# A hybrid decoder layer on one core: the fourth tile of the first queries moved into the stretch in which x lands

## The chip, the cores and the metric

The kernel runs on one core of one Trainium2 chip. The metric is device microseconds (us) of one execution, and the value to be predicted is the median over several executions of the changed kernel. The engines that matter here are TensorE (PE in the profile, with its weight loads as PEld), VectorE (DVE), ScalarE (ACT), GpSimd (POOL) and SyncE (SP), which issues most of the transfers.

## The reference, cut to what matters

One layer is computed for 512 tokens of width 1,024: a norm, one wide projection, gated linear attention, dilated attention in three groups, a merge, an MLP and a gated embedding. What the change touches is the first lines of it:

```
h = x * rsqrt(mean(x * x) + EPS) * ln1
q0, k0, q1, k1, ... = columns of h @ w_in      # group 0: queries q0, keys k0, four heads of 128 columns
logits0 = q0 @ k0^T / sqrt(128) + bias0        # needed later, once k0 and the bias tiles are there
```

## The kernel before

Every product of two fp32 matrices is made from three matmuls of a faster kind: each operand is split into a high part (`hi`, a copy on ACT) and a low part (`lo`, a subtraction on DVE), and high by high, high by low and low by high are added up in PSUM. A matmul here takes 128 rows of weights and streams 512 columns (the tokens).

**The start.** x arrives transposed, in eight chunks of 128 features by 512 tokens (`xr[k]`). Beside chunk k comes `wr[k]`, a piece of the tensor `ws`: the 128 rows of `w_in` for that chunk, for the first NS = 3 tiles (heads) of q0, and in a last column the norm's weight `ln1` for these features. SP issues ws 0, x 0, ws 1, x 1 and so on. For each k, ACT makes the high part of the weights (L465) and of x times `ln1` (L359) and a square of x (L390); DVE makes the low parts (L467, L367) and sums the squares (L472); PE then does 3 matmuls for each of the 3 tiles, which is 9 (L477 to L479, the second one of a tile needs the low part of x). The sum of squares is not needed yet: 1 / rms (`rstd`) is multiplied in when a finished tile is read out of PSUM (`qk0_evac`, L610). Eight matmuls on a tile of ones (L452) run before x is there.

**After the start.** The fourth tile of q0 and the four tiles of k0 are ordinary units: a weight tile `w` of 128 by 1,024 is loaded by SP (L201), split by `fetch` (L244 on ACT, L239 on DVE, up to two units ahead of use), and used by 24 matmuls in `fm` (L258). All of them use the splits of x that were made at the start.

**What sets the order.** The program is written out engine by engine in the order in which the Python code runs. `run` emits 8 matmuls and then calls `step`, which advances one of the generators in the list `side` by one yield. At this place `side` holds `setup` (the sum of squares into `rstd`: four small matmuls L397, a power on POOL, a diagonal tile that is split, and two matmuls L420 and L421 that spread it; then a small projection L560; then three small matmuls L577 for the bias tables, each with a copy on DVE, L579, and a store; then the loads that spread the tables into bias tiles, L595 and L597), and `renorm`, which makes for each of the eight chunks x times `ln1` times `rstd` (L497 on DVE), its high part (L357 on ACT) and its low part (L365 on DVE). From q1 on, all products use these normalized chunks `xs`. What is left in `side` after k0 is emitted by `drain()` in one piece, without matmuls between.

Each engine works its own list in order: an instruction that waits holds up all behind it on its engine. PSUM has eight banks, four for the large products (`mmt`) and four for small ones (`smt`), each handed out in turn.

```
side.append(setup())
q0t = fm("q0.3", xsr, ps=smt())
q0 = [qk0_evac(p, HD_SCALE) for p in q0ps + [q0t]]
k0 = [qk0_evac(fm(f"k0.{j}", xsr), 1.0) for j in range(4)]
drain()
side.append(xsums())
q1 = qk_cls("q1", HD_SCALE)
```

Of the kernel before, what the change touches and what calls it, by code (L numbers as in the profile page):

```python
# [10 lines left out]
F32 = mybir.dt.float32  # L11
F32R = mybir.dt.float32r
I32 = mybir.dt.int32
AF = mybir.ActivationFunctionType
OP = mybir.AluOpType
# [4 lines left out]
P = 128  # L20
T = 512
D = 1024
KC = D // P
EPS = 1e-6
NEG = -1e30
HD_SCALE = 128 ** -0.5


NS = 3


GQ, GK, GV, GR, GHA, ATT, GATE = 0, 512, 1024, 2048, 3072, 3088, 7696
# [2 lines left out]
def att_col(g, which):  # L35
    return ATT + (g * 3 + which) * 512
# [10 lines left out]
def weight_units():  # L47

    u = []

    def fm(name, src, col, n, row=0):
        for j in range(n):
            u.append((f"{name}.{j}", "fm", src, row, col + j * P))

    def tm(name, src, col):
        for i in range(4):
            u.append((f"{name}.{i}", "tm", src, i * 2 * P, col))

    fm("q0", "w_in", att_col(0, 0), 4)
    u = u[NS:]  # L60
    def quad(name, src, col, kind="quad", chunk=0):
        for m, k in ((0, 0), (1, 0), (1, 1), (0, 1)):
            u.append((f"{name}.A{m + 1}{k + 1}", kind, src, 2 * chunk + k, col + m * (P if kind == "quad" else 256)))

    fm("k0", "w_in", att_col(0, 1), 4)
    fm("q1", "w_in", att_col(1, 0), 4)
    quad("k1", "w_in", att_col(1, 1))
    quad("q2", "w_in", att_col(2, 0))
    quad("k2", "w_in", att_col(2, 1))
    quad("v1", "w_in", att_col(1, 2), "quadt")  # L70
    quad("v2", "w_in", att_col(2, 2), "quadt")
    quad("v0", "w_in", att_col(0, 2), "quadt")
    quad("gq", "w_in", GQ)
    quad("gk", "w_in", GK)
    quad("gv0", "w_in", GV, "quadt")
    for j in range(4):
        u.append((f"oa.{j}", "half", "w_o_attn", 0, j * 2 * P))
    quad("r0", "w_in", GR)
    quad("gv1", "w_in", GV + 512, "quadt")
    quad("r1", "w_in", GR + 512)  # L80
    for i in range(2):
        quad(f"gb{i}", "w_in", GATE + D + i * 512)
    for i in range(2):
        quad(f"ga{i}", "w_in", GATE + i * 512)
    fm("og", "w_o_gla", 0, 8)
    fm("wo", "w_out", 0, 8)
    for q in range(8):
        quad(f"m1q{q}", "w_mlp1", q * 512)
    for what, sub, c in MLP2:
        if what == "plain":  # L90
            for kk in range(4 * c, 4 * c + 4):
                u.append((f"m2s{sub}.{kk}", "tm", "w_mlp2", kk * 2 * P, sub * 512))
        else:
            quad(f"m2s{sub}c{c}", "w_mlp2", sub * 512, chunk=c)
    for j in range(2):
        u.append((f"pp{j}.0", "tm", "w_pp", 0, j * 512))
    for j in range(2):
        tm(f"pg{j}", "w_pg", j * 512)
    return u
# [35 lines left out]
C_LN2, C_LN3, C_BA, C_GN, C_LN1, C_LO, C_N = 0, 8, 16, 20, 28, 36, 38  # L135
# [14 lines left out]
def block_kernel(ctx, tc, xT, ws, pT, wts, wha, wa2, vec, lnf, rel, onehot, ident_d, mask_d, out):  # L150
    nc = tc.nc
    V, S, TE, SY, GP = nc.vector, nc.scalar, nc.tensor, nc.sync, nc.gpsimd

    const = ctx.enter_context(tc.tile_pool(name="const", bufs=1))
# [9 lines left out]
    def u32(name="u"):  # L164
        return ar.tile([P, T], F32, tag="u", name=name)
# [7 lines left out]
    def smt():  # L173
        return sm.tile([P, T], F32, tag="sm", name="smt")
# [76 lines left out]
    def weight(name, ahead=NW - 3):  # L251
        fetch(OPERAND[name] + ahead)
        return ready[name]
# [14 lines left out]
    def cols(t, c):  # L268
        return t[0][:, c], t[1][:, c]

    def fm(name, rhs, off=0, w=None, ps=None):

        w = w or weight(name)
        ps = ps or mmt()
        run(three(ps, [(cols(w, slice(off + i * P, off + (i + 1) * P)), rhs[i]) for i in range(len(rhs))]))
        return ps
# [151 lines left out]
    mh = const.tile([P, 4], F32, name="mh")  # L428
    V.memset(mh, -0.5)
    warm = const.tile([P, 4], F32, name="warm")  # L430
    S.activation(warm, mh, AF.Copy)
    xr, wr = [], []
    for k in range(KC):
        t = u32()
        SY.dma_start(t[:, 0:NS * P + 1], ws[k])
        wr.append(t)
        t = u32()
        SY.dma_start(t, xT[k * P:(k + 1) * P, :])
        xr.append(t)
    ident = const.tile([P, P], F32, name="ident")  # L440
    SY.dma_start(ident, ident_d)
    cv = const.tile([P, C_N], F32, name="cv")
    SY.dma_start(cv, vec)
    whs = const.tile([P, KC, 32], F32, name="whs")
    SY.dma_start(whs, wha)
    ones = const.tile([P, P], F32, name="ones")
# [11 lines left out]
    xsr = []  # L458
    acc, sq = None, None
    q0ps = [mmt() for _ in range(NS)]  # L460
    for k in range(KC):
        x, ln = xr[k], wr[k][:, NS * P:NS * P + 1]
        hi, lo = u32r(), u32r()
        c = slice(0, NS * P)
        S.activation(hi[:, c], wr[k][:, c], AF.Copy)  # L465
        xh = split_hi(x, ln)
        V.tensor_tensor(lo[:, c], wr[k][:, c], hi[:, c].bitcast(F32), op=OP.subtract)  # L467
        xsr.append(split_lo(x, xh, ln))
        if k == 1:
            acc = sq  # L470
        elif k > 1:
            V.tensor_tensor(acc, acc, sq, op=OP.add)  # L472
        sq = square(x)
        xh, xl = xsr[k]
        for i in range(NS):
            c = slice(i * P, (i + 1) * P)
            TE.matmul(q0ps[i], lhsT=hi[:, c], rhs=xh, start=k == 0, stop=False)  # L477
            TE.matmul(q0ps[i], lhsT=hi[:, c], rhs=xl, start=False, stop=False)  # L478
            TE.matmul(q0ps[i], lhsT=lo[:, c], rhs=xh, start=False, stop=k == KC - 1)  # L479
    V.tensor_tensor(acc, acc, sq, op=OP.add)  # L480
    for k in range(KC):
        V.tensor_scalar(whs[:, k, :], whs[:, k, :], wr[k][:, NS * P:NS * P + 1], None, op0=OP.mult)
    fetch(0)

    norm1, low, zin = [], [], []
# [121 lines left out]
    def qk0_evac(ps, scale):  # L607

        o = u32()
        V.scalar_tensor_tensor(out=o, in0=ps, scalar=scale, in1=norm1[1], op0=OP.mult, op1=OP.mult)  # L610
        return o
# [389 lines left out]


    side.append(setup())
    q0t = fm("q0.3", xsr, ps=smt())
    q0 = [qk0_evac(p, HD_SCALE) for p in q0ps + [q0t]]
    k0 = [qk0_evac(fm(f"k0.{j}", xsr), 1.0) for j in range(4)]
    drain()
    side.append(xsums())
    q1 = qk_cls("q1", HD_SCALE)
# [96 lines left out]
    for j in range(KC):  # L1106
        t = u32()
# [69 lines left out]
    for j in range(KC):  # L1177
        ps = fm(f"wo.{j}", mix)
# [166 lines left out]
    for i, (what, sub, c) in enumerate(MLP2):  # L1345
# [17 lines left out]
        if i == len(MLP2) - 2:  # L1363
            for k in range(2):
                t = u32()
                GP.dma_start(t, pT[k * P:(k + 1) * P, :])
                pt.append(split(t))
            for g in range(2):
                t = u32()
# [92 lines left out]
    for c in parts:  # L1462
        ps, n = mmt(), c.stop - c.start
# [37 lines left out]
def _layout(inputs):  # L1501
    f = {k: np.asarray(v) for k, v in inputs.items()}
    src = {k: f[k][0] for k in ("w_in", "w_o_gla", "w_o_attn", "w_out", "w_mlp1", "w_mlp2", "w_pp", "w_pg")}
    wts = np.empty((len(UNITS), P, 1024), np.float32)
    for i, (_, kind, s, r, c) in enumerate(UNITS):
        w = src[s]
        if kind == "fm":
            a = w[r:r + D, c:c + P].reshape(8, P, P).transpose(1, 0, 2)
        elif kind == "tm":
            a = w[r:r + 2 * P, c:c + 512].reshape(2, P, 512).transpose(1, 0, 2)  # L1510
        elif kind == "quadt":

            a = w.reshape(4, 2, P, -1)[:, r, :, c:c + 256].transpose(1, 0, 2)
        elif kind == "quad":

            a = w[r // 2 * D:(r // 2 + 1) * D].reshape(4, 2, P, -1)[:, r % 2, :, c:c + 3 * P]
            a = np.stack([a[..., :P], a[..., 2 * P:]], axis=2).transpose(1, 0, 2, 3)
        else:
            a = w[:, c:c + 256].reshape(4, P, 2, P).transpose(1, 2, 0, 3)
        wts[i] = a.reshape(P, 1024)  # L1520
    wha = np.zeros((P, KC, 32), np.float32)
    wha[:, :, :16] = src["w_in"][:, GHA:GHA + 16].reshape(KC, P, 16).transpose(1, 0, 2)
    wha[:, :, 16:] = wha[:, :, :16]
    wa2 = np.tile(f["w_a2"][0], (8, 1))
    vec = np.concatenate([v.reshape(-1, P).T for v in (f["ln2"][0], f["ln3"][0],
                                                       f["b_a"][0], f["gla_gn"][0], f["ln1"][0])]
                         + [np.tile(np.repeat(np.float32([[0, 1], [1, -1]]), 16, axis=0), (4, 1))], axis=1)
    c = att_col(0, 0)
    start = np.concatenate([src["w_in"][:, c:c + NS * P].reshape(KC, P, NS * P),
                            f["ln1"][0].reshape(KC, P, 1)], axis=2)  # L1530
    return {
        "xT": np.ascontiguousarray(f["x"][0].T),
        "ws": np.ascontiguousarray(start),
        "pT": np.ascontiguousarray(f["p"][0, 0].T),
        "wts": wts,
        "wha": wha,
        "wa2": wa2,
        "vec": np.ascontiguousarray(vec),
        "lnf": f["ln_f"].reshape(1, D),
        "rel": np.ascontiguousarray(f["rel_bias"]),  # L1540
        "onehot": _onehot(),
        "ident": np.eye(P, dtype=np.float32),
        "mask": np.triu(np.ones((P, P), np.int32)),
    }
# [16 lines left out]
```

## Time and profile before

| what | us |
|---|---|
| median of three runs | 968.62 |
| lowest and highest of them | 967.78, 969.78 |
| the profiled execution, its own time | 969.13 |
| span of its trace, first to last instruction | 967.3 |
| PE busy in that span | 958.1 (99%) |
| DVE busy | 745.7 (77%) |
| ACT busy | 538.1 (56%) |

The three runs lie within 2.0 us, or 0.2%, of each other. A busy time is a sum over an engine's instructions as the profile models them; matmuls overlap in the pipeline, so a PE that counts as busy can still be waiting inside a row. For that reason the distance from the start of one matmul to the start of the next tells more than its duration.

### The profile page before, as it was taken

To read this page: it belongs to the slowest core of one execution; us is meant where nothing else is said; L and a number is where in the kernel's file an instruction comes from. 1 tells how busy PE (TensorE), PEld (TensorE's weight loads), DVE (VectorE), ACT (ScalarE), POOL (GpSimd) and SP (SyncE) were. 2 spreads that over 40 slices of the span, in tenths; PEclk is the share of its full clock that TensorE was granted. 3 is DMA by queue.
4 is the path that set the end of the run, shared out by engine and by line. 5 is a ranking of instruction groups with operands and counts; after the bars stand their busy time and mean duration, and the time that the engine had idled before them with its cause. 6 is when DMAs were issued, how large, how long until landed. Compare 5 with 4: busy or idle time off the path is not lost.

```text
span 967.3 us, 16742 instructions
## 1 busy us (share of the span) xinstructions
PE 958.1 (99%) x6732; PEld 894.6 (92%) x6732; DVE 745.7 (77%) x1068; ACT 538.1 (56%) x878; POOL 103.6 (11%) x145
## 2 busy tenths in 40 slices
PE   9999999999999999999999999999999999999997
PEld 7789999999998999999988889999998998988886
DVE  7788879676788769977955788777767999787754
ACT  7347546445667667665732446555655664345633
POOL 0140010420001021013011000010000100000000
PEclk9999999999999999999999999999999999999999
DMA  8565555875446645455636427556664464563102
GB/s 295 156 202 127 153 134 130 235 200 134 110 109 186 163 116 146 116 148 176 175 92 208 118 62 195 153 137 169 160 168 109 111 177 106 133 195 108 44 1 88
DMA packets 41470, 138.93 MB, mean 144 GB/s; under 512 B 5363, under 2 KB 6975, under 8 KB 41392
## 3 DMA queue, kind: packets, MB, share of 16 engines
q1 hardware_dynamic: 27936, 93.29, 29.2%
q0 software_dynamic: 12160, 42.20, 22.1%
q10 hardware_dynamic: 1296, 2.36, 0.7%
q8 instruction: 53, 0.87, 0.4%
q14 instruction: 25, 0.20, 0.1%
HBM read 131.50 MB, written 8.17 MB: 144 GB/s over the span
## 4 chain that ended last, share of the span: by engine, by line
PE 95%; DVE 3%; issue 1%; ACT 1%; DMA 1%; SPq 0%; POOLq 0%; POOL 0%; DVEq 0%; ACTq 0%
PE mmt L258 82%; PE smt L258 4%; PE smt L863 1%; DVE ur L365 1%; PE smt L803 1%; PE smt L729 1%; DVE lo L239 1%; DMA u<-in_xT_dram 1%; PE mmt L478 1%; PE mmt L479 0%; PE mmt L477 0%; PE smt L700 0%; PE smt L820 0%; PE smt L809 0%; PE smt L819 0%
## 5 line engine op out<-in xcount | busy, mean ns | idle before, releaser
L258 PE MATMUL mmt<-ur,hi 128*128 128x256 f32 (+1 forms) x3152 | 647.3, 303 | 0.0
L258 PEld LDWEIGHTS mmt<-ur,hi 128*128 128x128 f32 x3152 | 505.8, 188 | 25.3 <-issue 1.9
L258 PE MATMUL mmt<-ur,lo 128*128 128x256 f32 (+1 forms) x1576 | 477.5, 303 | 0.8 <-DVE lo L239 0.8
L239 DVE TENSOR_TENSOR lo<-w,hi 128x1024 fp32r<-128x1024 f32 x251 | 304.3, 1219 | 51.8 <-PE mmt L258 32.7
L244 ACT ACTIVATE hi<-w 128x1024 fp32r<-128x1024 f32 x251 | 262.6, 1054 | 94.3 <-PE mmt L258 28.1
L258 PEld LDWEIGHTS mmt<-ur,lo 128*128 128x128 f32 x1576 | 297.1, 189 | 13.3 <-DVE lo L239 1.4
L258 PE MATMUL mmt<-hi,ur 128*128 128x256 f32 (+3 forms) x736 | 155.5, 306 | 0.0
L357 ACT ACTIVATE ur<-u 128x512 fp32r<-128x512 f32 x132 | 78.5, 624 | 104.0 <-DVE u L1098 30.7
L258 PEld LDWEIGHTS mmt<-hi,ur 128*128 128x128 f32 x736 | 118.9, 189 | 5.5
L258 PE MATMUL mmt<-lo,ur 128*128 128x256 f32 (+3 forms) x368 | 112.3, 305 | 0.0
L350 DVE TENSOR_TENSOR u<-u,mmt 128x512 f32<-128x512 f32 (+1 forms) x124 | 78.3, 656 | 43.4 <-PE mmt L258 43.3
L365 DVE TENSOR_TENSOR ur<-u,ur 128x512 fp32r<-128x512 f32 x131 | 86.2, 686 | 17.4 <-ACT ur L357 16.8
L332 ACT ACTIVATE u<-mmt 128x512 f32<-128x512 f32 x104 | 61.7, 593 | 57.9 <-PE mmt L258 57.8
L258 PEld LDWEIGHTS mmt<-lo,ur 128*128 128x128 f32 x368 | 69.4, 189 | 2.6
L221 POOL DMA_DIRECT2D w<-in_wts_dram x28 | 24.9, 889 | 356.3 <-DVE w L218 249.5
L210 POOL DMA_DIRECT2D w<-in_wts_dram x28 | 25.8, 920 | 279.0 <-DVE lo L239 51.4
L258 PE MATMUL smt<-ur,hi 128*128 128x512 f32 x144 | 44.7, 390 | 0.1
L218 DVE TENSOR_TENSOR w<-w 128x1024 f32<-128x1024 f32 x28 | 34.3, 1225 | 1.0
L224 DVE TENSOR_TENSOR w<-w 128x1024 f32<-128x1024 f32 x28 | 34.3, 1225 | 1.0
L258 PEld LDWEIGHTS smt<-ur,hi 128*128 128x128 f32 x144 | 26.9, 188 | 6.0 <-DVE ur L365 0.5
L258 PE MATMUL smt<-ur,lo 128*128 128x512 f32 x72 | 28.2, 391 | 0.0
L390 ACT ACTIVATE u<-u 128x512 f32<-128x512 f32 x24 | 14.9, 621 | 17.6 <-DVE u L1179 17.6
(210 smaller groups left out, 715.5 us busy)
## 6 DMA issues: line engine op xcount, KB each, us to landing
w<-in_wts_dram SPq DMA_DIRECT2D x167, 512.0 KB, 4.3
w<-in_wts_dram POOLq DMA_DIRECT2D x56, 512.0 KB, 5.8
u<-in_xT_dram SPq DMA_DIRECT2D x8, 256.0 KB, 5.0
v_dram<-u POOLq DMA_DIRECT2D x8, 256.0 KB, 6.9
u<-v_dram POOLq DMA_DIRECT2D x8, 256.0 KB, 7.7
y_dram<-u ACTq DMA_DIRECT2D x8, 256.0 KB, 2.3
u<-y_dram POOLq DMA_DIRECT2D x8, 256.0 KB, 7.8
u<-in_xT_dram POOLq DMA_DIRECT2D x8, 256.0 KB, 8.5
```

What stands on the lines that cost most here:

```text
L210: GP.dma_start(w, wts[UNIT[f"{q}.A22"]], accum_op=OP.add)
L218: V.tensor_tensor(w, w, raw[f"{q}.A11"], op=OP.add)
L221: GP.dma_start(w, wts[UNIT[f"{q}.A21"]], accum_op=OP.add)
L224: V.tensor_tensor(w, w, raw[f"{q}.A12"], op=OP.add)
L239: V.tensor_tensor(lo, w, hi.bitcast(F32), op=OP.subtract)
L244: S.activation(hi, w, AF.Copy)
L258: TE.matmul(o, lhsT=l, rhs=r, start=a, stop=b, skip_group_check=shared)
L332: S.activation(sums[c], bank[b], AF.Copy, scale=-scale if c[0] else scale)
L350: V.tensor_tensor(out, s, ps, op=OP.subtract if m else OP.add)
L357: S.activation(hi, x, AF.Copy)
L365: V.tensor_tensor(lo, x, hi.bitcast(F32), op=OP.subtract)
L390: S.activation(t, x, AF.Square, scale=1.0 / 32.0)
```

## The change

NS becomes 4, so `ws` brings all four tiles of q0 (512 columns a chunk in place of 384, and no `ln1` column), PE does 12 matmuls for each chunk at the start, and the unit q0.3 falls away (one weight tile less to load and to split, 24 matmuls less after the start; all in all the number of matmuls is the same, 6,563 rows in both programs). The column of `ln1` is now read from `cv`, a table of small vectors, whose load moves up to second place on SP. The first chunk of x is issued by ACT instead of SP, ahead of a small instruction (`warm`) that loads ACT's table. After the start, one `step()` is called, which emits the first part of `setup`; then k0.0 goes into a small bank, the q0 tiles are read out after it, and k0.1 goes into a small bank too, since all four large banks hold q0.

```
-NS = 3
+NS = 4
...
-    fm("q0", "w_in", att_col(0, 0), 4)
-    u = u[NS:]
...
-    S.activation(warm, mh, AF.Copy)
     xr, wr = [], []
+    cv = const.tile([P, C_N], F32, name="cv")
     for k in range(KC):
         t = u32()
-        SY.dma_start(t[:, 0:NS * P + 1], ws[k])
+        SY.dma_start(t, ws[k])
         wr.append(t)
+        if not k:
+            SY.dma_start(cv, vec)
         t = u32()
-        SY.dma_start(t, xT[k * P:(k + 1) * P, :])
+        (SY if k else S).dma_start(t, xT[k * P:(k + 1) * P, :])
         xr.append(t)
+    S.activation(warm, mh, AF.Copy)
     ident = const.tile([P, P], F32, name="ident")
     SY.dma_start(ident, ident_d)
-    cv = const.tile([P, C_N], F32, name="cv")
-    SY.dma_start(cv, vec)
...
-        x, ln = xr[k], wr[k][:, NS * P:NS * P + 1]
+        x, ln = xr[k], cv[:, C_LN1 + k:C_LN1 + k + 1]
...
     side.append(setup())
-    q0t = fm("q0.3", xsr, ps=smt())
-    q0 = [qk0_evac(p, HD_SCALE) for p in q0ps + [q0t]]
-    k0 = [qk0_evac(fm(f"k0.{j}", xsr), 1.0) for j in range(4)]
+    step()
+    k0ps = [fm("k0.0", xsr, ps=smt())]
+    q0 = [qk0_evac(p, HD_SCALE) for p in q0ps]
+    k0ps.append(fm("k0.1", xsr, ps=smt()))
+    k0 = [qk0_evac(p, 1.0) for p in k0ps]
+    k0 += [qk0_evac(fm(f"k0.{j}", xsr), 1.0) for j in (2, 3)]
     drain()
...
-    start = np.concatenate([src["w_in"][:, c:c + NS * P].reshape(KC, P, NS * P),
-                            f["ln1"][0].reshape(KC, P, 1)], axis=2)
+    start = src["w_in"][:, c:c + NS * P].reshape(KC, P, NS * P)
```

Fifteen calls of `step` lay between the start and `drain()` before (three in q0.3, twelve in k0); now there are thirteen. This shows at the end of k0. On PE, before, these rows stand around the third small matmul for the bias tables (L577, written to an `smt` bank); the `mmt` bank 570 is k0.3, and 648 is the first tile of q1.

```order
L258 MATMUL mmt_570<-ur_182,hi_408 128x512
L258 MATMUL mmt_570<-ur_185,hi_408 128x512
L577 MATMUL smt_579<-u_396,u_391 4x256
L258 MATMUL mmt_570<-ur_182,lo_460 128x512
L258 MATMUL mmt_570<-ur_202,hi_408 128x512
...
L258 MATMUL mmt_570<-ur_282,lo_460 128x512
L258 MATMUL mmt_648<-ur_423,hi_462 128x512
```

The third bias matmul stood after 8 of the 24 matmuls of k0.3, so 16 followed it before q1 began. In the changed program the same place of PE reads as follows (the line numbers are one or two lower; `mmt` bank 553 is k0.3, and 642 is the first tile of q1).

```order
L256 MATMUL mmt_553<-ur_304,hi_380 128x512
L256 MATMUL mmt_553<-ur_307,hi_380 128x512
L256 MATMUL mmt_553<-ur_304,lo_436 128x512
L576 MATMUL smt_589<-u_413,u_408 4x256
L256 MATMUL mmt_642<-ur_425,hi_438 128x512
L256 MATMUL mmt_642<-ur_473,hi_438 128x512
```

The third bias matmul has moved behind the whole of k0.3 and stands right ahead of q1. On DVE, before, the rows from that matmul's copy (L579) to the last of the normalized chunks were these; L610 is the read-out of k0.3, L497 and L365 belong to `renorm`.

```order
L579 COPY u_581<-smt_579 4x256
L497 SCALAR_TENSOR_TENSOR u_592<-u_106,cv_118,rstd_386 128x512
L365 TENSOR_TENSOR ur_596<-u_556,ur_558 128x512
L610 SCALAR_TENSOR_TENSOR u_611<-mmt_570,rstd_386 128x512
L497 SCALAR_TENSOR_TENSOR u_613<-u_110,cv_118,rstd_386 128x512
L365 TENSOR_TENSOR ur_617<-u_592,ur_594 128x512
L497 SCALAR_TENSOR_TENSOR u_635<-u_114,cv_118,rstd_386 128x512
L365 TENSOR_TENSOR ur_639<-u_613,ur_615 128x512
L365 TENSOR_TENSOR ur_641<-u_635,ur_637 128x512
```

Behind the read-out of k0.3 stood two L497 and three L365. In the changed program the same stretch of DVE reads as follows (L578 is the copy, L609 the read-out, L496 and L363 belong to `renorm`).

```order
L578 COPY u_591<-smt_589 4x256
L609 SCALAR_TENSOR_TENSOR u_594<-mmt_553,rstd_403 128x512
L496 SCALAR_TENSOR_TENSOR u_596<-u_107,cv_83,rstd_403 128x512
L363 TENSOR_TENSOR ur_600<-u_575,ur_577 128x512
L496 SCALAR_TENSOR_TENSOR u_607<-u_111,cv_83,rstd_403 128x512
L363 TENSOR_TENSOR ur_611<-u_596,ur_598 128x512
L496 SCALAR_TENSOR_TENSOR u_629<-u_115,cv_83,rstd_403 128x512
L363 TENSOR_TENSOR ur_633<-u_607,ur_609 128x512
L363 TENSOR_TENSOR ur_635<-u_629,ur_631 128x512
```

One more L496 and one more L363 stand behind the read-out of k0.3, and the copy of the third bias matmul now stands directly ahead of that read-out.

## Rows read from the trace of the kernel before

**Rows 1.** The page's chain of work that ended last: shares of the span by engine

```profile
PE 95%; DVE 3%; issue 1%; ACT 1%; DMA 1%; SPq 0%; POOLq 0%; POOL 0%; DVEq 0%; ACTq 0%
```

**Rows 2.** Timeline of PE at the start: start us, duration us, engine, line, operation, tiles

```profile
4.74 0.79 PE L477 MATMUL mmt<-ur 128*128 128x512 f32 x1
...
6.11 0.63 PE L479 MATMUL mmt<-ur 128*128 128x512 f32 x1
6.54 0.53 PE L477 MATMUL mmt<-ur 128*128 128x512 f32 x1
...
8.07 0.50 PE L477 MATMUL mmt<-ur 128*128 128x512 f32 x1
8.86 0.50 PE L478 MATMUL mmt<-ur 128*128 128x512 f32 x1 [0.28 <-DVE ur L367]
```

**Rows 3.** Chain that ended last, in order of time, first 9 us: start, length, what

```profile
2.12 5.16 DMA u<-in_xT_dram
...
8.05 0.76 DVE ur L367
```

**Rows 4.** Timelines of ACT and DVE at the start, chunk 0

```profile
3.24 0.52 ACT L465 ACTIVATE ur<-u 128x384 fp32r<-128x384 f32 x1 [0.81 <-DMA u<-in_ws_dram]
3.96 0.72 ACT L359 ACTIVATE ur<-u 128x512 fp32r<-128x512 f32 x1 [0.20 <-DMA u<-in_xT_dram]
...
4.72 0.75 DVE L367 SCALAR_TENSOR_TENSOR ur<-u,ur 128x512 fp32r<-128x512 f32 x1 [0.36 <-ACT ur L359]
```

**Rows 5.** SP's issues at the start, and the eight x loads from issue to landing

```profile
0.74 0.38 SPq L435 DMA_DIRECT2D u<-in_ws_dram  x1
1.18 0.42 SPq L438 DMA_DIRECT2D u<-in_xT_dram  x1
...
DMA to landing us min/median/max: 2.8/5.0/5.9
```

**Rows 6.** Stretches: us, busy of each engine, PEclk, DMA share, GB/s (last)

```profile
2.00:3.00 1.00, 1.00 (x7) 1.00 (x6) 0.00 (x0) 0.42 (x3) 0.00 (x0) 1.00 0.95 259
...
6.10:6.50 0.40, 0.40 (x2) 0.33 (x1) 0.00 (x0) 0.39 (x1) 0.00 (x0) 1.00 1.04 346
```

**Rows 7.** Timeline of PE, from the third bias matmul through the first tile of q1

```profile
52.02 0.59 PE L577 MATMUL smt<-u 33*4 33x256 f32 x2
52.54 0.50 PE L258 MATMUL mmt<-ur,lo 128*128 128x512 f32 x1
52.88 0.63 PE L258 MATMUL mmt<-ur,hi 128*128 128x512 f32 x2
...
56.30 0.62 PE L258 MATMUL mmt<-ur,hi 128*128 128x512 f32 x2
...
61.06 0.62 PE L258 MATMUL mmt<-ur,hi 128*128 128x512 f32 x2
```

**Rows 8.** Timeline of DVE, the same stretch

```profile
52.65 0.41 DVE L579 COPY u<-smt 4x256 f32<-4x256 f32 x1 [0.51 <-PE smt L577]
52.99 0.73 DVE L497 SCALAR_TENSOR_TENSOR u<-u,cv,rstd 128x512 f32<-128x512 f32 x1
...
56.50 0.69 DVE L610 SCALAR_TENSOR_TENSOR u<-mmt,rstd 128x512 f32<-128x512 f32 x1 [2.18 <-PE mmt L258]
57.11 0.74 DVE L497 SCALAR_TENSOR_TENSOR u<-u,cv,rstd 128x512 f32<-128x512 f32 x1
...
58.37 0.74 DVE L497 SCALAR_TENSOR_TENSOR u<-u,cv,rstd 128x512 f32<-128x512 f32 x1
59.03 1.47 DVE L365 TENSOR_TENSOR ur<-u,ur 128x512 fp32r<-128x512 f32 x2
```

**Rows 9.** The bias tiles: last loads on POOL, their landing time, first use on DVE

```profile
68.84 1.06 POOL L597 DMA_DIRECT2D u<-cb_dram  x2
...
u<-cb_dram POOLq DMA_DIRECT2D x8, 64.0 KB, 5.5
...
82.25 0.28 DVE L676 TENSOR_TENSOR u<-smt,u 128x128 f32<-128x128 f32 x1
```

More of the change, by code (lines that the diff above doesn't have):

```diff
@@ L481, in block_kernel @@
     for k in range(KC):
-        V.tensor_scalar(whs[:, k, :], whs[:, k, :], wr[k][:, NS * P:NS * P + 1], None, op0=OP.mult)
+        V.tensor_scalar(whs[:, k, :], whs[:, k, :], cv[:, C_LN1 + k:C_LN1 + k + 1], None, op0=OP.mult)
     fetch(0)
```

## The prediction

> **What bounds the kernel now.** I read the chain of work that ended last first. PE holds 95% of it [rows 1], so a change is worth what it adds to or takes from PE's time, and only where PE runs out of work. So I went on to the timeline of PE, looking for distances between the starts of neighbouring matmuls that are longer than the work. In full flow 21 matmuls of 512 columns take 61.06 - 56.30 = 4.76 us [rows 7], which is 0.227 us each.
>
> At the start the distances are longer. Chunk 0's nine matmuls run from 4.74 to 8.07 [rows 2], 0.37 each. Chunk 1's first matmul starts at 8.07, needs 0.23, and the next starts only at 8.86: PE waits 8.86 - 8.30 = 0.56 us. The chain says for what: x 1 was issued at 2.12 and took 5.16 us to land, then ACT made its high part, and DVE its low part from 8.05 to 8.81 [rows 3]. From 8.86 on the timeline shows no further wait for a chunk: the loads run ahead of PE. So at the start the kernel is bound by x 0 and x 1, and behind that by the number of matmuls.
>
> The second place is the start of q1. Its first tile uses the eight normalized chunks in turn. The last low part is made by the second of two L365 that end at 59.03 + 1.47 = 60.50 [rows 8]. The matmul that needs it is the second of chunk 7, at 61.06 + 0.23 = 61.29 [rows 7]. PE doesn't wait there, but the cover is only 0.79 us.
>
> **The change: matmuls.** Nothing is saved in number: 24 matmuls move from behind the start into it, 3 for each chunk. They can gain only what they fill of PE's waits.
>
> **The start.** Before, 10 matmuls were done at 8.86 and 62 + 24 were left. After, with chunk 0 complete and chunk 1 begun, 13 are done and 83 are left: 3 x 0.227 = 0.68 us less behind the wait, if the wait ends at the same moment. Two things move it.
>
> PE's beginning: ws 0 is 65 KB larger (127 columns of 4 bytes in 128 rows); at the 259 GB/s of that stretch [rows 6] that is 0.25 us. Its high part has 512 columns for 384, so at most 0.52 x 4/3 = 0.69 us. It began at 3.24 [rows 4]: now it ends between 3.93 and 4.18, and the high part of x 0, which began at 3.96, starts between 3.96 and 4.18. DVE's low part is next on the same chain (4.72 [rows 4]) and moves along. I take 0.15 later, so PE begins at 4.89. Chunk 0 then ends at 8.07 + 0.68 + 0.15 = 8.90, and chunk 1's first matmul at 9.13.
>
> The wait's end: SP issues x 1 in the same place of its list as before (ws 0, cv, ws 1, x 1), but 2 x 65 + 19 = 149 KB more lie ahead of it; at 346 GB/s [rows 6] that is 0.43 us. The second matmul of chunk 1 starts between 9.13 and 9.29. I take 9.20. The start gains 0.68 - (9.20 - 8.86) = **0.34 us**.
>
> Bounds. Best: the whole wait of 0.56 goes, and everything moves ahead by the 0.44 us between SP's first two issues [rows 5], since x 0 no longer stands second: 1.00. Worst: x 1 takes 5.9 us, the slowest of the eight [rows 5], in place of 5.16; the wait ends 0.74 later, and 0.68 - 0.74 is a loss of 0.06.
>
> One rule speaks against the part with the other queue. The Trainium skill, DMA: Bandwidth & Descriptors, section Issuing engines are not separate DMA queues, says that transfers issued by different engines run on the same 16 DMA engines and interleave, so that a second issuer saves only issue time. By that page, 0.44 us would be the most that ACT's issue of x 0 can bring. My sum gives it nothing for a reason in the rows: ws 0, now larger, is needed ahead of x 0 [rows 4]. No row of before shows two issuers at the start.
>
> **ACT and DVE at the start.** The extra 128 columns cost ACT at most 0.17 us a chunk, while PE's time for a chunk grows by 0.68, so both fall less behind PE, not more. The table load that now stands behind ACT's issue of x 0 has the time up to 3.24, when ACT last waited for a load [rows 4]. cv must be there by 4.18: it is 19 KB and second in the queue, where x 0 landed in time for 3.96. If it came later, all of PE's beginning would move by as much.
>
> **After the start.** `setup` begins ahead of k0.0 instead of 8 matmuls into q0.3; between its four small matmuls and the two that spread `rstd` there are 16 matmuls as before, 3.6 us, so no new wait. Two splits on ACT (1,024 columns, by the 384-column one at most 1.4 us each) now come ahead of the copy of `rstd`, so the q0 read-outs come up to 2.8 us later against PE. Nothing asks for them until k0.2 takes q0's first bank, 24 matmuls of k0.1 later (5.4 us). Without that cover it would be 2.8 us.
>
> **The start of q1.** Thirteen steps stand where fifteen did, so `renorm` is behind when `drain()` comes. One more L496 and L363 now follow the read-out of k0.3: the pair takes 58.37 - 57.11 = 1.26 us [rows 8]. And the third bias matmul has moved to directly ahead of q1. Its copy stands ahead of that read-out on DVE and holds up all of `renorm` behind it. Before, the matmul had PE until 52.54, the copy started at 52.65 and DVE went on at 52.99 [rows 7, 8], so the read-out now starts 0.45 after q1's first matmul; before it was 56.50 - 56.30 = 0.20. That is 0.25 more, and 1.51 in sum. The first matmul behind a bias matmul takes 52.88 - 52.54 = 0.34 in place of 0.23 [rows 7], so q1 asks 0.11 later. PE waits 1.51 - 0.11 - 0.79 = **0.61 us**, most of it for chunk 6's low part, the rest for chunk 7's. Bounds: nothing, if DVE gets through sooner than in this one execution; 1.2 us if another pair falls behind. Behind DVE's delay stand the splits for the later tiles of q1, made two tiles (48 matmuls, 10.9 us) ahead: hidden.
>
> The bias tables end later by the 16 matmuls that used to follow, 3.6 us, and so do the loads of the bias tiles: the last were issued by 69.90 and took 5.5 [rows 9], so 75.4 becomes 79.0. DVE first adds a bias tile at 82.25 [rows 9], and that first tile was loaded first. Hidden, with 3 us over even for the last.
>
> **Sum.** -0.34 + 0.61 = +0.27 us. On the profiled execution (969.13 for a span of 967.3) that is 969.40; it stands 0.51 above the median, so the forecast is 968.62 + 0.27 = **968.9 us**.
>
> **The rivals.** (A) The cover at q1 holds: no wait there, and the start gains 0.34 to 1.00, so 967.6 to 968.3. For it: DVE idles 2.18 us right ahead of the read-out [rows 8], so it is not short of time. Against: that idle time lies ahead of the copy, which all of `renorm` stands behind. (B) The start gives nothing: x 1 lands as late as the slowest chunk, a loss of 0.06, and q1 waits 0.61 to 1.2, so 969.3 to 969.9. For it: x 1's landing set the wait before, and more bytes lie ahead of it. (C) The clock, on the other side. Between 6.11 and 6.54 a matmul took 0.43 us [rows 2], 512 columns at 1.2 GHz; in full flow they take 0.227, the 2.4 GHz level (the granted clock reads 1.00 in all these stretches [rows 6], so the level is read from the distances). The warm-up matmuls reached up to chunk 0 before. If PE falls idle ahead of a later chunk 0 and the low level lasts longer, each matmul in it costs 0.20 more: up to 11.0 instead of some 6.9 that is (11.0 - 6.9) / 0.43 = 9.5 matmuls, 1.9 us, and 968.9 + 1.9 = 970.8. It passes the bound for slower from 8.4 such matmuls, a rise at about 10.5. Against it: PE begins only 0.15 later in my sum. The Trainium skill, TensorE: Matmul & The Clock Gate, section What's actually happening, says that PE's clock is gated to half until the engine has been busy; the distances here agree.
>
> That the change doesn't do what it says (q0.3 computed in PE's wait) is ruled out in the order of instructions, and only its price is open.
>
> **How the numbers follow.** Forecast 0.58, A 0.20, B 0.15, C 0.07. The three runs before lie within 0.2% of each other, which is about what a measurement of this kernel can tell from no change: 966.7 to 970.6. Forecast, A and B lie inside it, C outside: within 0.93; a little of that goes to the ends for the scatter of the runs, so faster 0.02, same 0.90, slower 0.08. The range takes in A and B and the 1 us by which single runs lay off the median, most of it at the upper end: 967.2 to 970.5.
>
> **What would show it.** In the trace after: chunk 0's twelve matmuls without a gap and at most 0.2 us of wait ahead of chunk 1's second matmul, which starts at 9.13 to 9.29; q1's first tile with a distance of about 0.5 us too much at chunk 6's second matmul, released by DVE's L363; the third copy at the start of q1; the span within 1 us of 967.3. The prediction is wrong if distances of 0.43 last beyond 9 us, if cv lands after 4.2, if the spread of `rstd` waits, or if PE waits in k0 for something that I held to be hidden.

## The result, and the profile after

The changed kernel takes 969.85 us (median of 22 runs, lowest 968.91) and the kernel before 968.18 (22 runs, 967.70 to 969.78). The ratio is 1.0016, with a 95% interval of 1.0009 to 1.0022: slower by a little, and inside what was called no change. The forecast was 968.9. The profiled execution took 970.67 for a span of 968.9.

The times of the changed kernel are not spread evenly. Two of the 22 lie far off (1303.75 and 2102.27) and stand outside the ratio; 11 lie at 968.91 to 969.64 (median 969.09) and 9 at 970.06 to 971.28 (median 970.67). So the median, 969.85, is the middle of the gap between them, and no execution took that time. The profile below is of the second group.

The chain of work that ended last, by engine, answers to [rows 1]: PE still holds 95%, DMA has gone from 1% to 0%.

```profile
PE 95%; DVE 3%; issue 1%; ACT 1%; DMA 0%; POOLq 0%; POOL 0%; DVEq 0%; ACTq 0%
```

The timeline of PE at the start (start us, duration us, engine, line, operation, tiles, in brackets the idle time ahead and who ended it) answers to [rows 2]:

```profile
1.00 3.78 PE L451 MATMUL smt<-ones 128*128 128x128 f32 x16 [1.00 <-POOL ones L446]
5.74 0.80 PE L476 MATMUL mmt<-ur 128*128 128x512 f32 x1 [0.96 <-ACT ur L357]
...
7.12 0.63 PE L478 MATMUL mmt<-ur 128*128 128x512 f32 x1
7.54 0.63 PE L476 MATMUL mmt<-ur 128*128 128x512 f32 x1
...
9.25 0.63 PE L477 MATMUL mmt<-ur 128*128 128x512 f32 x1
9.68 0.50 PE L478 MATMUL mmt<-ur 128*128 128x512 f32 x1
...
10.71 0.40 PE L476 MATMUL mmt<-ur 128*128 128x512 f32 x1
10.94 0.39 PE L477 MATMUL mmt<-ur 128*128 128x512 f32 x1
```

Three things are to be seen. PE begins at 5.74, 1.00 later than before, and for 0.96 us ahead of that it stands idle behind the warm-up. The distance from 7.12 to 7.54, or 9.25 to 9.68, is 0.43, the 1.2 GHz level; it lasts up to 9.68, where before it ended by 6.9. And the wait for x 1 is gone: chunk 1's second matmul (10.94) follows its first at 0.23. That second matmul is the 14th of the start. In the timeline of PE before, the 14th is this row, three behind the one at 8.86 of [rows 2]:

```profile
9.66 0.40 PE L478 MATMUL mmt<-ur 128*128 128x512 f32 x1
```

So the changed kernel is 10.94 - 9.66 = 1.28 us late there, where the forecast had it 0.34 early.

The timeline of ACT answers to [rows 4]. ACTq is ACT's issue of x 0. Behind it stands cv's row in the trace's list of transfers: KB, and us from issue to landing.

```profile
0.74 0.40 ACTq L438 DMA_DIRECT2D u<-in_xT_dram  x1
...
4.44 0.63 ACT L464 ACTIVATE ur<-u 128x512 fp32r<-128x512 f32 x1 [1.56 <-DMA u<-in_ws_dram]
4.98 0.71 ACT L357 ACTIVATE ur<-u,cv 128x512 fp32r<-128x512 f32 x1
...
6.92 0.72 ACT L357 ACTIVATE ur<-u,cv 128x512 fp32r<-128x512 f32 x1 [0.20 <-DMA u<-in_xT_dram]
```

```profile
cv<-in_vec_dram SPq DMA_DIRECT2D x1, 19.0 KB, 3.6
```

PE begins late because ACT waits for ws 0 until 4.44; before it was 3.24. x 0 and cv are there by 4.98, since ACT doesn't wait for them. cv is so only just: issued at 1.19, it landed at about 4.8, and it cost nothing because ACT was still at work on the late ws 0. x 1 is there at 6.92.

At the start of q1, the timelines of DVE and then of PE answer to [rows 8] and [rows 7]:

```profile
57.53 0.41 DVE L578 COPY u<-smt 4x256 f32<-4x256 f32 x1 [2.71 <-PE smt L576]
57.87 0.67 DVE L609 SCALAR_TENSOR_TENSOR u<-mmt,rstd 128x512 f32<-128x512 f32 x1
```

```profile
57.42 0.73 PE L256 MATMUL mmt<-ur,hi 128*128 128x512 f32 x2
...
58.22 0.62 PE L256 MATMUL mmt<-ur,hi 128*128 128x512 f32 x2
...
61.69 0.40 PE L256 MATMUL mmt<-ur,hi 128*128 128x512 f32 x1
62.38 0.50 PE L256 MATMUL mmt<-ur,hi 128*128 128x512 f32 x1 [0.30 <-DVE ur L363]
62.72 0.40 PE L256 MATMUL mmt<-ur,lo 128*128 128x512 f32 x1
62.96 0.72 PE L256 MATMUL mmt<-ur,hi 128*128 128x512 f32 x2
63.51 0.40 PE L256 MATMUL mmt<-ur,lo 128*128 128x512 f32 x1
```

The copy of the third bias table now holds up the read-out on DVE until 57.87, 0.45 behind q1's first matmul (57.42), and PE waits for the low part of chunk 6: from 61.69 to 62.38 is 0.69 where 0.23 is work. From chunk 1's first matmul (58.22) to chunk 7's third (63.51) are 20 matmuls, 5.29 us; at 0.227 they take 4.54. PE loses 0.75.

### The profile page after: what moved, and what is told of

Read it like the earlier page. It is cut to its first block, busy times and chain, and to the rows that moved or that the text cites. A ratio compares the mean times of both kernels' runs of the same rounds, so it can differ in the third digit from the quotient of the medians.

```text
span 968.9 us, 16740 instructions
## 1 busy us (share of the span) xinstructions
PE 958.7 (99%) x6732; PEld 894.9 (92%) x6732; DVE 745.1 (77%) x1067; ACT 537.6 (55%) x877; POOL 103.7 (11%) x145
## 4 chain that ended last, share of the span: by engine, by line
PE 95%; DVE 3%; issue 1%; ACT 1%; DMA 0%; POOLq 0%; POOL 0%; DVEq 0%; ACTq 0%
PE mmt L256 80%; PE smt L256 5%; PE smt L862 1%; DVE ur L363 1%; PE mmt L477 1%; PE mmt L476 1%; PE mmt L478 1%; PE smt L802 1%; PE smt L728 1%; DVE lo L237 1%; DMA u<-in_ws_dram 0%; PE smt L819 0%; PE smt L699 0%; PE smt L808 0%; PE smt L818 0%
## 5 line engine op out<-in xcount | busy, mean ns | idle before, releaser
L256 PE MATMUL mmt<-ur,hi 128*128 128x256 f32 (+1 forms) x3120 | 637.4, 302 | 0.3 <-DVE ur L363 0.3
L256 PEld LDWEIGHTS mmt<-ur,hi 128*128 128x128 f32 x3120 | 500.2, 188 | 24.2 <-DVE ur L363 1.2
L256 PE MATMUL mmt<-ur,lo 128*128 128x256 f32 (+1 forms) x1560 | 471.2, 302 | 0.8 <-DVE lo L237 0.8
L256 PEld LDWEIGHTS mmt<-ur,lo 128*128 128x128 f32 x1560 | 294.0, 188 | 12.4 <-DVE lo L237 1.2
L363 DVE TENSOR_TENSOR ur<-u,ur 128x512 fp32r<-128x512 f32 x131 | 86.1, 684 | 16.8 <-ACT ur L355 16.2
L256 PE MATMUL smt<-ur,hi 128*128 128x512 f32 x160 | 49.9, 391 | 0.1
L256 PEld LDWEIGHTS smt<-ur,hi 128*128 128x128 f32 x160 | 29.8, 188 | 6.6 <-DVE ur L363 0.5
L256 PE MATMUL smt<-ur,lo 128*128 128x512 f32 x80 | 31.3, 391 | 0.0
```

What stands on the lines that cost most here:

```text
L256: TE.matmul(o, lhsT=l, rhs=r, start=a, stop=b, skip_group_check=shared)
L363: V.tensor_tensor(lo, x, hi.bitcast(F32), op=OP.subtract)
```

## The experiments

Four theories are at stake, each of which bears a letter here and in the expectations. **Q**: x 0 on ACT's queue makes ws 0 late. **P**: cv ahead of x 0 makes x 0 late. **G**: the clock rises at a moment that varies from execution to execution; where PE goes idle behind the warm-up before that moment, the rise can come some 3 us later (here behind 9.68, before by 6.9), and that makes the two groups of times. Its rival is that the landing of the loads makes them. **D**: thirteen steps where there were fifteen make the wait at q1.

**1. x 0 back on SP (e1).** In the changed kernel, SP issues ws 0, cv, x 0.

```
-        (SY if k else S).dma_start(t, xT[k * P:(k + 1) * P, :])
+        SY.dma_start(t, xT[k * P:(k + 1) * P, :])
```

> The changed kernel, with x 0 issued by SP again (third in its list: ws 0, cv, x 0, ws 1). Theory Q (the other queue): ws 0 landed at 4.44 us in place of 3.24 because x 0 from a second queue shares the DMA engines with it; alone it lands by 3.6, PE begins by 5.1, and the time falls by 0.7 to 2.5 us against the changed kernel (969.85), to 967.4 to 969.1. Rival S (the larger ws 0 and cv, not the queue): ws 0 still lands after 4.1 and the time stays within 0.5 of 969.85.

Measured: 971.78 (971.31 to 972.56, 5 runs), ratio 1.0038 (1.0026 to 1.0051). Timelines of ACT and of PE:

```profile
3.50 0.63 ACT L464 ACTIVATE ur<-u 128x512 fp32r<-128x512 f32 x1 [1.06 <-DMA u<-in_ws_dram]
5.61 0.72 ACT L357 ACTIVATE ur<-u,cv 128x512 fp32r<-128x512 f32 x1 [1.48 <-DMA u<-in_xT_dram]
```

```profile
6.38 0.50 PE L476 MATMUL mmt<-ur 128*128 128x512 f32 x1 [1.92 <-ACT ur L357]
...
10.56 0.52 PE L476 MATMUL mmt<-ur 128*128 128x512 f32 x1
```

ws 0 is there at 3.50 instead of 4.44, as Q says; but x 0, third now, comes at 5.61, and PE begins still later, after 1.92 us of idling. The time is 1.9 us above the changed kernel's 969.85, where Q had expected it 0.7 to 2.5 below. So Q is right on ws 0 and missed the time: with cv in second place, ACT's issue of x 0 was a gain on balance.

**2. cv second in the kernel before (e7).** Nothing else is changed: `SY.dma_start(cv, vec)` moves to between ws 0 and x 0.

> The kernel before, with one edit: SP issues cv second, between ws 0 and x 0 (three tiles, the norm's column still from ws). Theory P (the third load on SP's queue lands late): x 0 lands at 5.2 to 5.8 in place of 3.9, PE begins after 5.9, and the time rises by 0.8 to 3.5. Rival B (cv is 19 KB and costs its bytes alone): x 0 lands by 4.4 and the time is within 0.4 of the kernel before.

Measured: 970.45 (968.45 to 971.30, 10 runs), ratio 1.0017 (1.0008 to 1.0026). Timelines of SP and of ACT:

```profile
1.65 0.42 SPq L441 DMA_DIRECT2D u<-in_xT_dram  x1
```

```profile
5.16 0.72 ACT L359 ACTIVATE ur<-u 128x512 fp32r<-128x512 f32 x1 [1.41 <-DMA u<-in_xT_dram]
```

P holds: a load of 19 KB ahead of x 0 makes it 5.16 - 3.96 = 1.20 us later [rows 4]. 0.47 of that is the issue, since SP comes to x 0 at 1.65 instead of 1.18 [rows 5]; for the other 0.73 the bytes, 0.07 at 259 GB/s [rows 6], are far too few. By the ratio (1.0017) this one move costs as much as the whole change (1.0016). By the medians it is 970.45 - 968.37 = 2.1 us, but its runs too fall into two groups, four at 968.45 to 969.33 and six at 970.30 to 971.30, and the median falls in the larger one.

**3. x 0 by ACT in the kernel before (e4).** Again alone, with the `warm` instruction behind it as in the change.

```
-        SY.dma_start(t, xT[k * P:(k + 1) * P, :])
+        (SY if k else S).dma_start(t, xT[k * P:(k + 1) * P, :])
```

> The kernel before, with one part of the change alone: x 0 issued by ACT ahead of its table load (three tiles, ws with the norm's column, all else as before). Theory Q (the other queue): ws 0 lands after 3.9 in place of 3.24, PE begins 0.5 to 1.0 later, and the time rises by 0.5 to 2.0 over the kernel before, more than half of what the whole change cost. Rival S (size of ws 0 and cv): ws 0 lands by 3.4, x 0 sooner than 3.9, and the time is within 0.3 of the kernel before, or up to 0.4 below it.

Measured: 968.69 (967.79 to 970.45, 11 runs), ratio 1.0010 (1.0001 to 1.0019). Seven runs lie at 967.79 to 969.26, four at 970.11 to 970.45. Timeline of ACT:

```profile
4.71 0.52 ACT L465 ACTIVATE ur<-u 128x384 fp32r<-128x384 f32 x1 [1.83 <-DMA u<-in_ws_dram]
```

Q is shown: ws 0 of the old size lands at 4.71, 1.47 later than before, so its delay doesn't come from its 65 KB more. The profiled execution (968.34) had 0.23 distances from 7.03 on, though PE idled 1.12 us ahead of chunk 0: the gap makes the late rise possible, not certain. The price is at the low end of what was expected (0.5 to 2.0): 0.5 by the medians (968.18 before), and a ratio of 1.0010 where the whole change has 1.0016.

**4. The two steps back (e2).** In the changed kernel, fifteen steps stand ahead of q1 again.

```
-    k0 += [qk0_evac(fm(f"k0.{j}", xsr), 1.0) for j in (2, 3)]
+    for j in (2, 3):
+        step()
+        k0.append(qk0_evac(fm(f"k0.{j}", xsr), 1.0))
```

> The changed kernel, with one more step ahead of k0.2 and one ahead of k0.3, so that fifteen steps stand before the drain again and the third bias matmul is back behind 8 matmuls of k0.3. Theory D (the late renorm holds up q1): PE's wait of about 0.6 us in the first tile of q1 goes, and the time falls by 0.6, to 969.2; the start is as in the changed kernel. Rival N (the wait there is made up for by a later wait that it hides): the wait goes, and the time stays within 0.2 of 969.85.

Measured: 970.00 (968.29 to 970.70, 11 runs), ratio 1.0013 (1.0004 to 1.0022); four runs at 968.29 to 968.86, seven at 969.7 to 970.7. The median is not the 969.2 that D expected; taken by itself it fits rival N (within 0.2 of 969.85). It hides the gain because more runs fell in the upper group; group against group, a sorting made after the fact, it is 0.5 to 0.8. In the timeline of PE the wait in q1's first tile is gone: its first matmul starts at 57.55 and chunk 7's first, 21 matmuls on, at 62.31, which is 4.76 as before [rows 7]. That D makes the wait is shown by this; what the wait costs is shown cleanly by experiment 7 beside 5.

**5. A longer warm-up (e3).** In the changed kernel, NWARM goes from 8 to 11: 22 passes on the tile of ones in place of 16 (the trace shows two passes for each of these matmuls).

> The changed kernel, with 11 warm-up matmuls in place of 8, which reach to about 5.9 us, past the first matmul on x (5.74). Theory G (PE's gap of 1.0 us ahead of chunk 0 made the clock rise late, so that nine matmuls took 0.43 us): no gap, distances of 0.23 by 7.5 us, and the time falls by 0.8 to 1.6, to 968.3 to 969.1, without the two groups of runs (969.1 and 970.7) of the changed kernel. Rival R (the moment of the rise is chance, whatever PE does before): distances of 0.43 beyond 8 us in some executions still, both groups of runs remain, and the median stays within 0.5 of 969.85.

Measured: 969.14 (968.92 to 969.84, 11 runs), ratio 1.0011 (1.0002 to 1.0020). Ten of the 11 lie within what was the lower group, and the eleventh, 969.84, is still under the upper one. Timeline of PE:

```profile
0.99 4.06 PE L451 MATMUL smt<-ones 128*128 128x128 f32 x22 [0.99 <-POOL ones L446]
5.64 0.50 PE L476 MATMUL mmt<-ur 128*128 128x512 f32 x1 [0.59 <-ACT ur L357]
6.43 0.50 PE L477 MATMUL mmt<-ur 128*128 128x512 f32 x1 [0.29 <-DVE ur L365]
6.76 0.40 PE L478 MATMUL mmt<-ur 128*128 128x512 f32 x1
7.00 0.39 PE L476 MATMUL mmt<-ur 128*128 128x512 f32 x1
```

22 passes took 4.06 us where 16 took 3.78: the last ones ran at the higher level, so the clock rose within the warm-up, and an idle time of 0.59 behind it didn't bring it down. No gap at all had been expected. The loads are issued as in the changed kernel, and chunk 0 began nearly as late (5.64), yet the upper group is gone. That the landing of the loads doesn't make it is seen more directly by setting two executions side by side. First e2's, with x 1 there early, and then that of experiment 7, where ACT waits longest for x 1: timelines of ACT and of PE for each.

```profile
6.57 0.71 ACT L357 ACTIVATE ur<-u,cv 128x512 fp32r<-128x512 f32 x1
```

```profile
9.18 0.63 PE L477 MATMUL mmt<-ur 128*128 128x512 f32 x1
9.61 0.54 PE L478 MATMUL mmt<-ur 128*128 128x512 f32 x1
```

```profile
7.34 0.72 ACT L357 ACTIVATE ur<-u,cv 128x512 fp32r<-128x512 f32 x1 [0.56 <-DMA u<-in_xT_dram]
```

```profile
7.14 0.40 PE L476 MATMUL mmt<-ur 128*128 128x512 f32 x1
7.37 0.40 PE L477 MATMUL mmt<-ur 128*128 128x512 f32 x1
```

e2 with the early loads is at the low level up to 9.61, and experiment 7's execution with the late ones is at the high level by 7.14.

**6. The changed kernel twice more (e11, e12).** No edit. If G is right, time and clock go together.

> The changed kernel once more, one look. Its runs fell at about 969.1 or about 970.7, and the profile shown was of the upper group (970.67). Theory G: time and clock go together: a run near 969.1 has distances of 0.23 from about 7 on, and a run near 970.7 has 0.43 up to about 9.7. Rival (the groups come from something else, later in the kernel): a run near 969.1 with 0.43 up to 9.7, or one near 970.7 with 0.23 from 7 on.

> The same kernel and the same question once more, since one look has an even chance to fall in the group that has been seen: near 969.1 with 0.23 from about 7 on, or near 970.7 with 0.43 up to about 9.7 by theory G; any other pairing speaks against it.

Measured: 969.07 and 970.84, one of each group. Timelines of PE, first of 969.07 and then of 970.84:

```profile
5.69 0.50 PE L476 MATMUL mmt<-ur 128*128 128x512 f32 x1 [0.91 <-ACT ur L357]
...
6.81 0.40 PE L478 MATMUL mmt<-ur 128*128 128x512 f32 x1
7.04 0.40 PE L476 MATMUL mmt<-ur 128*128 128x512 f32 x1
...
9.34 0.39 PE L477 MATMUL mmt<-ur 128*128 128x512 f32 x1
```

```profile
5.79 0.80 PE L476 MATMUL mmt<-ur 128*128 128x512 f32 x1 [1.00 <-ACT ur L357]
...
7.17 0.63 PE L478 MATMUL mmt<-ur 128*128 128x512 f32 x1
...
9.73 0.63 PE L478 MATMUL mmt<-ur 128*128 128x512 f32 x1
10.15 0.49 PE L476 MATMUL mmt<-ur 128*128 128x512 f32 x1
```

One program, the same loads: chunk 0 begins 0.10 apart, the third matmul is 0.36 apart, and the spans (967.3 and 969.1) differ by 1.8. All of it is there by the 14th matmul (9.34 and 11.18), so nothing later makes the groups. This is the direct evidence for G. The trace's own records of the granted clock say the same: the first one at full clock starts at 4.94 in the execution of 969.07, while PE was idle, and at 10.37 in the other. In all the traces that have a gap of PE behind the warm-up, that first record starts either by 5.45 (e1, e3, e4, e6, e8, e11) or from 9.90 on (the changed kernel's profile, e2, e5, e7, e12), never between. Each of the latter five took at least 970.00, each of the former but e1, which lost the high level again, at most 969.07. The 14th matmul of the faster one starts at 9.34, 0.32 ahead of before's 9.66, although PE began 0.95 late: without the low level and without a wait for x 1, the start is a gain.

**7. Both repairs (e6).** The edits of e2 and e3 together.

> The changed kernel with both repairs of the earlier runs: fifteen steps and 11 warm-up matmuls; the loads as changed (ws 0 and cv by SP, x 0 by ACT). Theories G and D (each repair takes its own share): 969.14 of the warm-up run less 0.62 for q1's wait gives 968.5, in one narrow group of runs, 0.2 to 0.5 above the kernel before, since ws 0 still lands 1.2 late. Rival N (the shares are not additive, the wait returns elsewhere): 968.9 to 969.3.

Measured: 968.51 (968.14 to 969.10, 11 runs) beside 968.37 for the kernel before; ratio 1.0001 (0.9992 to 1.0010). G and D add up, and with both repairs no loss is left that the interval can tell from nothing. Beside e3, which has the longer warm-up alone and no upper group either, the two steps are worth 969.14 - 968.51 = 0.63, and nine of these 11 runs lie under e3's lowest: that is D's price without any sorting. In the timeline of PE, chunk 7 of q1's first tile begins at 60.81, where it was 61.06 before [rows 7], and nothing waits there:

```profile
60.81 0.62 PE L256 MATMUL mmt<-ur,hi 128*128 128x512 f32 x2
```

**8. Other places for cv (e5, e8, e9).** In all three SP issues ws 0, x 0, ws 1 and so on, with four tiles and fifteen steps. In e5 POOL issues cv, in e8 ACT ahead of its table load, and e9 is e8 with NWARM 10.

```
-            SY.dma_start(cv, vec)
+            S.dma_start(cv, vec)
```

> Four tiles, fifteen steps, 8 warm-up matmuls; SP issues ws 0, x 0, ws 1, x 1 in the old order, and POOL issues cv behind its first memset. Theory P (x 0 needs the second place on SP, and a small load elsewhere does not hold up ws 0): ws 0 by 3.6, x 0 by 4.4, PE begins by 5.2 without a gap over 0.7, and the time is 0.2 to 0.8 below the kernel before, 967.4 to 968.0. Rival M (any second issuer at the start holds up the first loads): ws 0 after 4.1 or x 0 after 4.8, and 968.4 to 970.5.

> As the run with cv by POOL, but ACT issues cv ahead of its table load. Theory P: ws 0 by 3.6, x 0 by 4.4, 967.4 to 968.0. Rival M: ws 0 after 4.1 or x 0 after 4.8, and 968.4 to 970.5.

> The start with ws 0 and x 0 by SP and cv by ACT, fifteen steps, and now 20 passes of warm-up in place of 16. Of its 11 runs with 16 passes 8 lay at 968.0 to 968.8 and 3 at 969.66 to 970.41. Theory G (the clock rises at a moment that varies; where the warm-up ends before it and PE falls idle, it rises only some 3 us later): with the longer warm-up the upper group goes; median 968.2, none above 969.3, and x matmuls 0.23 apart from the third on. The kernel before stood at 968.2 to 968.4, so the two are within 0.05% of each other. Rival (the upper group comes from where the loads land): 2 to 4 of 11 runs still above 969.5, median 968.7.

Measured: e5 970.62 (969.08 to 972.02, 11 runs), ratio 1.0021 (1.0012 to 1.0030); e8 968.70 (968.00 to 970.41, 11 runs), ratio 1.0006 (0.9997 to 1.0015); e9 968.05 (967.83 to 968.38, 11 runs), before 968.20, ratio 0.9999 (0.9990 to 1.0008). P had expected 967.4 to 968.0 of both e5 and e8. Timelines of ACT, of e5 and then of e8:

```profile
5.64 0.72 ACT L357 ACTIVATE ur<-u,cv 128x512 fp32r<-128x512 f32 x1 [1.51 <-DMA cv<-in_vec_dram]
```

```profile
4.53 0.72 ACT L357 ACTIVATE ur<-u,cv 128x512 fp32r<-128x512 f32 x1 [0.18 <-DMA u<-in_xT_dram]
```

By POOL, cv itself came too late, which neither side had said. By ACT, all three loads of chunk 0 are there by 4.53, ws 0 by 3.72, but the time was not below the kernel before's. Three of e8's 11 runs were still at 969.66 to 970.41; with the longer warm-up none of e9's is above 968.38. That is what G says, and the narrowest spread of all.

**9. The longer warm-up in the kernel before (e10).** NWARM 11.

> The kernel before with 22 passes of warm-up in place of 16. Theory G: here PE goes from the warm-up into chunk 0 without a gap, and the late rise (distances of 0.43 up to 6.9 in the profiled execution) is hidden ahead of the wait for x 1 that ends at 8.86; so the median stays within 0.3 us of the kernel before on the same chip, with a narrower spread than its 967.6 to 969.9. Rival (the low level costs the kernel before too): over 0.5 us faster. A loss over 0.5 us would say that the warm-up itself is in the way of chunk 0.

Measured: 968.02 (967.33 to 968.75, 11 runs) beside 968.20 (967.55 to 969.60); ratio 0.9996 (0.9987 to 1.0005). No gain that can be told, a somewhat narrower spread. Timeline of PE:

```profile
8.01 0.50 PE L478 MATMUL mmt<-ur 128*128 128x512 f32 x1
```

Here the wait for x 1 ended at 8.01, where the profiled execution of the kernel before had 8.86 [rows 2], with the loads in the same order. The wait on which the prediction built its gain differs that much between executions.

## Why the prediction was right, and where a step failed

The number was right to within 0.95 us and the sign and the range held, but luck has a large part in it. The loss forecast was 0.27 us; measured by the medians it is 969.85 - 968.18 = 1.67. That this shows as only 0.95 comes from the kernel before, whose median over 22 runs is 0.44 lower than over the three that the forecast started from. The median lies within the range only as the middle of two groups. The 11 executions of the lower one (969.09) are near the forecast, though 0.91 above the kernel before; the other 9 did what rival C said, and seven of them lie above the range. In the profile two of the prediction's own signs of being wrong came true: distances of 0.43 beyond 9 us, and cv landing after 4.2, at about 4.8.

- **PE's beginning** (4.89 forecast, 5.74 measured) is the step that failed. I gave ACT's issue of x 0 nothing, for better or worse, and made ws 0 later by its extra bytes alone, 0.25 at most. It was 1.20 later. Experiments 1 and 3 show that ACT's issue of x 0 did it: with x 0 issued by ACT ws 0 landed between 4.34 and 4.71 in all seven such traces, with x 0 on SP between 3.23 and 3.72 in seven. The Trainium skill, DMA: Bandwidth & Descriptors, section Issuing engines are not separate DMA queues, says that transfers of different issuers interleave on the same 16 DMA engines. The traces agree: ws 0 and x 0 are now issued in the same moment (0.74), and land at 4.44 and 0.74 + 3.9 = 4.64, where they landed by 3.24 and 3.96 [rows 4]. It goes on that a second issuer saves only issue time. Here not even that was gained: x 0 was issued 0.44 earlier and landed 0.68 later. The price that my sum lacked stands in the same rows: ws 0, which used to land first, landed 1.20 late. The row of x 0 in the trace's list of transfers, with KB and us from issue to landing:

```profile
u<-in_xT_dram ACTq DMA_DIRECT2D x1, 256.0 KB, 3.9
```

- **The clock.** Against rival C I held that PE begins only 0.15 later. With 1.00 that argument was gone. C had the mechanism, and its 970.8 stands beside the group's 970.7; but it came to that with a low level up to 11.0 and 1.9 us on top of 968.9, where the low level lasted to 9.7 to 10.2 and the groups lie 1.6 apart. That the two meet so closely is partly chance.
- **The wait for x 1** was put at 9.20. It vanished: x 1 was there at 6.92 in this profile, and in e11 its high part started at 6.58 without a wait. In e11 this made up for the late beginning: the 14th matmul started at 9.34 where I had 9.20, and the start gained 0.32 where I had 0.34. Two errors, in the beginning and in the wait, cancel there, so that the term came out right in this execution is luck.
- **The start of q1** (0.61) was right in place and cause. 0.75 was measured: 0.46 ahead of chunk 6's second matmul, 0.10 in chunk 7, 0.11 because the matmul behind the wait takes 0.34 in place of 0.23 (62.38 to 62.72 in the rows of PE after), and the rest in small pieces. The 0.11 and the pieces I had not counted.
- **The bias copies, the spread of `rstd`, the q0 read-outs:** no wait of PE for them, as said.
- **The sum.** In e11, where the clock rises early, it can be checked by rows: the timeline of PE at the start of q1 shows chunk 1's first matmul, chunk 7's first two, and chunk 7's third.

```profile
56.62 0.62 PE L256 MATMUL mmt<-ur,hi 128*128 128x512 f32 x2
...
61.35 0.72 PE L256 MATMUL mmt<-ur,hi 128*128 128x512 f32 x2
61.91 0.40 PE L256 MATMUL mmt<-ur,lo 128*128 128x512 f32 x1
```

Before, chunk 1 began at 56.30 + 3 x 0.227 = 56.98 and chunk 7's third matmul at 61.06 + 2 x 0.227 = 61.51 [rows 7]. So e11 comes to q1 0.36 early and leaves the tile 0.40 late: -0.36 + 0.76 = +0.40, where the forecast's sum was +0.27. At the end the two spans are equal (967.3). Most of the 0.4 us between is not the change's: the profiled execution of the kernel before, which I had put at 0.51 above its median and which is 0.95 above that of the 22 runs, lost it. The timelines show where. DVE waited there 4.10 us for a load of y, until 446.35 (2.85 in e10, whose program is the same behind the warm-up). Its next splits of weights came late, and PE lost time at two of them: three matmuls each, from 452.76 to 453.39 and from 455.89 to 456.39, take 0.63 and 0.50 where e10 has 0.36. Across this stretch the execution fell 0.43 back against e10, and DVE's rows show 0.36 against e11 and as much against e6. Why the load of y was late in it stays open.

Open are two causes: what sets the moment at which the clock rises, and why 19 KB in second place on a queue cost the next transfer 0.7 us beyond its later issue. The runs show both effects and no mechanism.

## What to carry to other kernels

Ask of a load that is moved to another queue which load was landing first until then, and who needs it: here x 0 came no sooner on the second queue (4.64 after 3.96), and ws 0, which is needed ahead of it, came 1.2 us later. Ask of anything that delays PE's first real matmul whether the warm-up still reaches it; a few more passes on the tile of ones (16 to 20 or 22) took away a group of runs 1.6 us slower. And look at single times before the median: two groups 1.6 us apart, with hardly a run between, say that something switches.

## What the runs showed that was not expected

The clock rose at a different moment in executions with the same work up to there. In e3 the passes of the warm-up came closer within its 4.06 us, in the kernel before the distances of 0.43 lasted to about 6.5, in the changed kernel to about 9.7 or not beyond 6.8 (e11). In e1 16 passes took 3.48 us instead of 3.78, so the clock had risen in the warm-up too; 1.92 us of idling followed, and from 7.57 the distances were 0.43 again until 10.56. There the granted clock shows the level too: 0.50 in the stretch from 9 to 10, the third number from the end of the second row here. Ahead of the first rise it reads 1.00 whatever the distances are, as in [rows 6], because the trace has no record of the clock from that time; there only the distances between matmuls tell the level.

```profile
0.99 3.48 PE L451 MATMUL smt<-ones 128*128 128x128 f32 x16 [0.99 <-POOL ones L446]
```

```profile
9.00:10.00 1.00, 1.00 (x4) 0.81 (x3) 0.94 (x2) 1.00 (x3) 0.00 (x0) 0.50 1.04 399
```

A small load ahead of a large one made it 1.2 us later (e7: 19 KB, 0.47 of it by the later issue). By the traces' lists of transfers the same 19 KB took 4.3 us from issue to landing on POOL's queue (e5), 3.1 on ACT's (e8), and in second place on SP's 2.2 (e7) or 3.6 (the changed kernel), where the fastest x load, 256 KB, took 2.8 [rows 5].
